# Softmax in a two-layer encoder trunk: dividing the value products instead of the probabilities, with reciprocals brought over the rows through DRAM

## The chip, the cores and the metric

The kernel runs on one core of a Trainium2 chip. The metric is device time in microseconds (us). Six places do the work: TensorE (PE, matmuls and transposes; PEld is its weight load), VectorE (DVE), ScalarE (ACT), GpSimd (POOL), SyncE (SP, which here issues every DMA) and the DMA engines. Each engine takes its own instructions in order; they wait for each other through semaphores.

## The reference

Two layers, 512 tokens, width 1024. Each layer has three attention branches of 8 heads with 64-wide values, a gated sum of them, and a feed-forward part. What matters here is the softmax and what follows it, the same in all branches:

```python
p = jax.nn.softmax(jnp.where(mask, s, NEG_INF), axis=-1)
outs.append(jnp.einsum('bhqk,bkhd->bqhd', p.astype(v.dtype), v[:, :q1]))
...
proj = jnp.einsum('bsnc,ncd->bsnd', y, w_branch[l])
gates = jax.nn.sigmoid(gl + b_gate[l]).reshape(B, S, N_BRANCH, D_MODEL)
merged = jnp.sum(gates * proj, axis=2)
x = x + merged @ w_out[l]
```

Branch 0 masks frame by frame and adds a forgetting bias, branch 1 (latent attention) masks by chunk, branch 2 adds a relative-position bias.

## The kernel before, in words

Matrix operands are kept as pairs: a rounded high part and the remainder ("hi"/"lo", `whi`/`wlo`, `yh`/`yl`), so that one product is three matmuls. Each weight tile is loaded by SP (`raw`), rounded by ACT (`whi`, L140) and its remainder taken by DVE or POOL (`wlo`, L142), with three buffers of each.

In a layer the branches come in the order 0, 2, 1. Attention goes head by head. For head h, `scores` handles four blocks of 128 queries in the order i = 3, 2, 1, 0 (512 to 128 keys each): PE makes `ps_s`; in branch 0 POOL first adds the diagonal mask to the bias tile `cb` (L665); DVE adds bias and score and takes the row's extreme (L670); ACT takes the exponential and its row sum `ls` (L675); DVE takes the reciprocal of the sum (L676) and multiplies the block of probabilities `pr` by it (L677). Then `probs` transposes the blocks on PE (`ps_p`, L689) and ACT and DVE split them (`pth` L691, `ptl` L692); `values` multiplies them with the values (`ps_y`, L700), so that features stand on partitions and queries on columns. The upper half of `ps_y` holds the low part of the values; ACT copies it (L704), DVE adds it (L709) and writes 64 partitions of the pair's tile `y`. After the odd head of a pair, ACT rounds it to `yh` (L712) and DVE takes the rest `yl` (L713). The next pair's queries and keys are transposed (`ps_q` L583), split (`nat` L585 on ACT, L586 on DVE) and, in branches 0 and 2, stacked by 12 DMAs (`qq`, `kk`, `kl`, L598). `nat` has three buffers, and a pair needs four, so that the fourth split waits until `qq` has read the first.

The order of the work on PE is written out by hand (the table `seq` in TUNE): scores of head h are interleaved with transposes and value products of head h-1, and between any two steps `Fill` puts matmuls that do not depend on the softmax: gate projections (`ps_f`) and branch projections (`ps_b`). On the other engines and in SP's queue the order is set by a scheduler that places instructions by its own estimates of times. Scratch tiles of 128x512 (`tmp`, shown as `t`) rotate through six buffers.

Of the kernel before, what the change touches and what calls it, by code (L numbers as in the profile page):

```python
# [9 lines left out]
F32 = mybir.dt.float32  # L10
# [3 lines left out]
ALU = mybir.AluOpType  # L14
# [4 lines left out]
P = 128  # L19
T = 512  # L20
# [4 lines left out]
H = 8  # L25
HD = 64
# [46 lines left out]
    head=1.0,  # L73
# [104 lines left out]
class Kern:  # L178
# [409 lines left out]
    def stacked(self, which, h, lo):  # L588
# [4 lines left out]
        def over(tag, first, second):  # L593
            s = self.tk(tag, [P, 2, T], F32R)
            for u in range(2):
                own, other = slice(HD * u, HD * u + HD), slice(HD - HD * u, P - HD * u)
                for rows, x in ((own, first), (other, second)):
                    nc.sync.dma_start(out=s[rows, u].bitcast(F32), in_=x[own].bitcast(F32))  # L598
            return s
# [2 lines left out]
            return over("kk", h, h), over("kl", lo, lo)  # L602
        return over("qq", h, lo), None

    def attention(self, l, branch, fill_ns, qkv):

        nc = self.nc
        yh, yl = [], []
        self.y = (yh, yl)
        per = 1 if branch == 1 else 2  # L610
        rows = KB if branch == 1 else P
        gc = (V_GA, V_GB, V_GC)[branch]
        qk, head = {}, {}
        if branch == 1:
            maskb = self.tk("maskb", [P, T], F32)
            nc.gpsimd.memset(maskb, 0.0)
            nc.gpsimd.memset(maskb[0:64, 448:512], BIG)
        else:
            cb = [self.tk("cb", [P, T], F32) for _ in range(2)]
        if branch == 2:  # L620
            for c in cb:
                nc.gpsimd.memset(c[0:64, 448:T], -BIG)

        def src(x, u):
            if branch == 1:
                return lambda t: x[t // 2][:, t % 2, u, :]
            return lambda t: x[t // 2][:, t % 2, u * P : (u + 1) * P]

        def transposed(u, which):
            x = qkv[which]  # L630
            if branch == 1:
                parts = [self.tk("st", [P, T], F32R) for _ in range(2)]
            else:
                parts = [self.tk("nat", [P, T], F32R) for _ in range(2)]
            self.feature_major(src(x, u), rows, self.gain(l, gc + which, 0, rows), parts)
            qk[u, which] = parts if branch == 1 else self.stacked(which, *parts)

        def begin(h):
            if branch == 1:
                bias = maskb  # L640
            else:
                bias = cb[h % 2]
                if branch == 0:
                    nc.sync.dma_start(out=bias, in_=self.cum[h : h + 1, :].to_broadcast([P, T]))
                else:
                    nc.sync.dma_start(out=bias[:, 0:448], in_=self.a["rel"][l, h, :, 0:448])
                    nc.sync.dma_start(out=bias[64:P, 448:T], in_=self.a["rel"][l, h, 64:P, 448:T])
            head[h] = dict(bias=bias, p=self.tk("pr", [P, 10 * P], F32))

        def scores(h, i):  # L650
            s = head[h]
            (qh, ql), (kh, kl) = qk[h // per, 0], qk[h // per, 1]
            if branch == 1:
                terms = [(a[0:KB], b[0:KB]) for a, b in ((qh, kh), (qh, kl), (ql, kh))]
            else:
                u = h % 2
                terms = [(qh[:, u], kh[:, u]), (qh[:, u], kl[:, u])]
            n = P * (i + 1)
            off = P * (i * (i + 1) // 2)
            ps = self.pS.tile([P, T], F32, tag="s", name="ps_s")  # L660
            for j, (a, b) in enumerate(terms):
                nc.tensor.matmul(out=ps[:, 0:n], lhsT=a[:, i * P : (i + 1) * P], rhs=b[:, 0:n], start=j == 0, stop=j == len(terms) - 1)  # L662
            if branch == 0:
                d = s["bias"][:, n - P : n]
                nc.gpsimd.tensor_tensor(out=d, in0=d, in1=self.maska, op=ALU.add)  # L665
            p = s["p"][:, off : off + n]
            b = s["bias"][:, 0:n] if branch == 0 else s["bias"][:, T - n : T]
            mn, ls, li = (self.small(1, x, 6) for x in ("mn", "ls", "li"))
            sign = 1.0 if branch == 2 else -1.0
            nc.vector.tensor_tensor_reduce(out=p, in0=ps[:, 0:n], in1=b, scale=1.0, scalar=-3e38 * sign, op0=ALU.add, op1=ALU.max if branch == 2 else ALU.min, accum_out=mn)  # L670
            if branch == 2:
                nm = self.small(1, "nm", 4)
                nc.vector.tensor_scalar(out=nm, in0=mn, scalar1=-1.0, scalar2=None, op0=ALU.mult)
                mn = nm
            nc.scalar.activation(out=p, in_=p, func=AF.Exp, bias=mn, scale=sign, accum_out=ls)  # L675
            nc.vector.reciprocal(out=li, in_=ls)  # L676
            nc.vector.tensor_scalar(out=p, in0=p, scalar1=li, scalar2=None, op0=ALU.mult)  # L677

        groups = (((0, 0),), ((1, 0), (3, 384)), ((2, 0),))
        offs = [0, P, 3 * P, 6 * P]  # L680

        def probs(h, gi):
            pr = head[h]["p"]
            ps = self.pt.tile([P, T], F32, tag="pt", name="ps_p")
            w = max(o + (NT - kb) * P for kb, o in groups[gi])
            for i in range(NT - 1, -1, -1):
                for kb, o in groups[gi]:
                    if kb <= i:
                        nc.tensor.transpose(ps[:, o + (i - kb) * P : o + (i - kb + 1) * P], pr[:, offs[i] + kb * P : offs[i] + (kb + 1) * P], self.ident)  # L689
            ph, pl = self.tk("pth", [P, T], F32R), self.tk("ptl", [P, T], F32R)  # L690
            nc.scalar.activation(out=ph[:, 0:w], in_=ps[:, 0:w], func=AF.Copy)  # L691
            nc.vector.tensor_tensor(out=pl[:, 0:w], in0=ps[:, 0:w], in1=ph[:, 0:w].bitcast(F32), op=ALU.subtract)  # L692
            head[h][gi] = (ph, pl)

        def values(h, gi, x):
            if gi == 0 and x == 0:
                head[h]["y"] = self.py.tile([P, T], F32, tag="y", name="ps_y")
            yps = head[h]["y"]
            for j, (kb, o) in enumerate(groups[gi]):
                nc.tensor.matmul(out=yps[:, kb * P : T], lhsT=qkv[2][kb // 2][:, kb % 2, h, :], rhs=head[h][gi][x][:, o : o + T - kb * P], start=gi == 0 and x == 0, stop=gi == 2 and x == 1)  # L700
            if gi < 2 or x == 0:
                return
            half = self.tmp()
            nc.scalar.activation(out=half[0:HD], in_=yps[HD:P], func=AF.Copy)  # L704
            if h % 2 == 0:
                head["y"] = self.tmp()
            y = head["y"]
            r0 = HD * (h % 2)
            nc.vector.tensor_tensor(out=y[r0 : r0 + HD], in0=yps[0:HD], in1=half[0:HD], op=ALU.add)  # L709
            if h % 2 == 1:  # L710
                a, b = self.ypool.tile([P, T], F32R, tag="yh", name="yh", bufs=4), self.ypool.tile([P, T], F32R, tag="yl", name="yl", bufs=4)
                nc.scalar.activation(out=a, in_=y, func=AF.Copy)  # L712
                nc.vector.tensor_tensor(out=b, in0=y, in1=a.bitcast(F32), op=ALU.subtract)  # L713
                yh.append(a)
                yl.append(b)
            del head[h]

        step = {
            "S": lambda h, i: scores(h, i),
            "P": lambda h, g: probs(h - 1, g),  # L720
            "V": lambda h, gx: values(h - 1, gx // 10, gx % 10),
            "T": lambda h, w: transposed(h // per + 1, w),
        }
        plan = []
        for h in range(H + 1):
            for op, arg, ns in TUNE["seq"]:
                if op == "T" and not (h % per == 0 and h // per + 1 < H // per):
                    continue
                if op == "S" and h == H or op in "PV" and h == 0:
                    continue  # L730
                plan.append((h, op, arg, ns * (TUNE["tail"] if h == H else TUNE["head"] if h == 0 else 1.0)))
        scale = fill_ns / sum(x[3] for x in plan)
        transposed(0, 0)
        yield 0.0
        transposed(0, 1)
        yield 0.0
        at = -1
        for h, op, arg, ns in plan:
            if h != at and h < H:
                begin(h)  # L740
            at = h
            step[op](h, arg)
            yield ns * scale
# [361 lines left out]
```

## Time and profile before

| | |
|---|---|
| median of three runs | 1857.61 us (1857.18 to 1859.98) |
| the profiled execution | 1858.96 us |
| its span, first to last instruction | 1856.9 us |
| mean granted TensorE clock | 0.993 |
| PE busy / DVE / ACT / POOL | 97% / 59% / 42% / 17% |

The page gives busy time by engine. The stretches of the attention branches are read off the timeline (times from the start of the span): in the first layer branch 0 stands at 74 to 178 us, branch 2 at 239 to 342, branch 1 at 437 to 513; in the second layer branch 0 at 995 to 1101, branch 2 at 1162 to 1265, branch 1 at 1362 to 1438. In the timelines and wait lists an idle time stands in square brackets or ahead of "times", with what ended it. "issue" of a DMA is the time that SP takes for it; "landing" is from issue until its data is there.

### The profile page before, as it was taken

The numbers are of one execution on the slowest core, as the hardware profiler recorded it, in microseconds if no ns is written. First come the engines' busy times: TensorE is split into PE (matmuls) and PEld (weight loads), VectorE is DVE, ScalarE is ACT, GpSimd is POOL, SyncE is SP. The second block draws the span as 40 slices with busy tenths as digits, with TensorE's granted clock in tenths as the row PEclk, the third lists the DMA queues.
The fourth block names the chain that finished last, engine by engine and source line by source line (L and its number), as shares of the span: only waits on it lengthen the run. The fifth ranks groups of instructions, "written<-read, shape, count | busy, mean of one in ns | idle before, by whom it ended". The sixth has DMA issues, their size and how long they took to land.

```text
span 1856.9 us, 23295 instructions
## 1 busy us (share of the span) xinstructions
PE 1801.5 (97%) x8496; PEld 1495.0 (81%) x8496; DVE 1088.9 (59%) x2223; ACT 784.5 (42%) x1369; POOL 311.4 (17%) x289
## 2 busy tenths in 40 slices
PE   8989989989999999999999899899899999999999
PEld 6778878877888888888887788788778888888887
DVE  7566468488865642454355654684888756334632
ACT  6565456446643221223245644564466433222221
POOL 1442222043101000000124312220431110000000
PEclk9999999999999999999999999999899999999999
DMA  5653365332252333333336533643322533333341
GB/s 180 154 147 105 101 163 138 100 113 69 80 193 80 106 99 98 96 100 110 119 113 158 132 96 109 169 116 110 103 84 80 178 95 97 102 91 102 92 119 62
DMA packets 78850, 211.46 MB, mean 114 GB/s; under 512 B 11392, under 2 KB 14464, under 8 KB 78736
## 3 DMA queue, kind: packets, MB, share of 16 engines
q1 hardware_dynamic: 78736, 209.97, 39.3%
q8 instruction: 67, 1.10, 0.2%
q14 instruction: 47, 0.39, 0.1%
HBM read 172.15 MB, written 12.62 MB: 100 GB/s over the span
## 4 chain that ended last, share of the span: by engine, by line
PE 79%; DVE 8%; ACT 4%; DMA 4%; issue 3%; POOL 2%; SPq 1%; DVEq 0%; ACTq 0%; POOLq 0%
PE ps L331 38%; PE ps_t L366 15%; PE ps_f L331 10%; PE ps_o L331 5%; PE ps_b L776 5%; PE ps_s L662 2%; PE ps_p L689 2%; PE ps_y L700 2%; DMA qq<-nat 2%; DVE pr L677 1%; POOL wlo L142 1%; DVE pr L670 1%; ACT whi L140 1%; DMA cb<-cum 1%; ACT pr L675 1%
## 5 line engine op out<-in xcount | busy, mean ns | idle before, releaser
L140 ACT ACTIVATE whi<-raw 128x1024 fp32r<-128x1024 f32 (+1 forms) x337 | 307.1, 919 | 764.8 <-issue 320.6
L142 DVE TENSOR_TENSOR wlo<-raw,whi 128x1024 fp32r<-128x1024 f32 (+2 forms) x237 | 287.6, 1213 | 232.2 <-ACT whi L140 227.8
L331 PE MATMUL ps<-xgh,whi 128*128 128x512 f32 x512 | 199.4, 389 | 0.0
L331 PE MATMUL ps<-xgh,wlo 128*128 128x512 f32 x512 | 199.2, 389 | 0.0
L331 PE MATMUL ps<-xgl,whi 128*128 128x512 f32 x512 | 199.2, 389 | 0.0
L331 PE MATMUL ps<-ah,whi 128*128 128x512 f32 x512 | 199.2, 389 | 0.0
L331 PE MATMUL ps<-al,whi 128*128 128x512 f32 x512 | 199.2, 389 | 0.0
L331 PE MATMUL ps<-ah,wlo 128*128 128x512 f32 x512 | 199.2, 389 | 0.0
L331 PE MATMUL ps_f<-xgh,whi 128*128 128x512 f32 x464 | 196.2, 423 | 0.0
L331 PE MATMUL ps_f<-xgh,wlo 128*128 128x512 f32 x464 | 182.5, 393 | 0.0
L331 PE MATMUL ps_f<-xgl,whi 128*128 128x512 f32 x464 | 182.5, 393 | 0.0
L142 POOL TENSOR_TENSOR wlo<-raw,whi 128x1024 fp32r<-128x1024 f32 x50 | 121.1, 2422 | 257.0 <-ACT whi L140 234.3
L366 PE MATMUL ps_t<-whi,xgh 128*128 128x512 f32 x384 | 151.2, 394 | 7.0 <-ACT whi L140 7.0
L366 PE MATMUL ps_t<-wlo,xgh 128*128 128x512 f32 x384 | 150.1, 391 | 0.0
L366 PE MATMUL ps_t<-whi,xgl 128*128 128x512 f32 x384 | 149.9, 390 | 0.0
L283 POOL TENSOR_TENSOR acc<-acc,t 128x512 f32<-128x512 f32 x24 | 41.6, 1732 | 518.9 <-ACT t L282 518.9
L331 PEld LDWEIGHTS ps<-ah,whi 128*128 128x128 f32 x512 | 96.1, 188 | 20.1
L331 PEld LDWEIGHTS ps<-xgl,whi 128*128 128x128 f32 x512 | 96.1, 188 | 19.9
L331 PEld LDWEIGHTS ps<-xgh,wlo 128*128 128x128 f32 x512 | 96.1, 188 | 19.9
L331 PEld LDWEIGHTS ps<-al,whi 128*128 128x128 f32 x512 | 96.1, 188 | 19.9
L331 PEld LDWEIGHTS ps<-xgh,whi 128*128 128x128 f32 x512 | 96.1, 188 | 19.9
L331 PEld LDWEIGHTS ps<-ah,wlo 128*128 128x128 f32 x512 | 96.1, 188 | 19.8
(194 smaller groups left out, 3387.0 us busy)
## 6 DMA issues: line engine op xcount, KB each, us to landing
raw<-w SPq DMA_DIRECT2D x277, 512.0 KB, 3.6
qq<-nat SPq DMA_DIRECT2D x64, 128.0 KB, 2.9
kk<-nat SPq DMA_DIRECT2D x64, 128.0 KB, 2.4
kl<-nat SPq DMA_DIRECT2D x64, 128.0 KB, 2.4
gd<-t SPq DMA_DIRECT2D x32, 256.0 KB, 2.2
cb<-cum SPq DMA_DIRECT2D x16, 256.0 KB, 4.0
cb<-gd SPq DMA_DIRECT2D x16, 256.0 KB, 2.7
g<-gd SPq DMA_DIRECT2D x16, 256.0 KB, 4.3
```

The costliest lines, as they stand in the source:

```text
L140: nc.scalar.activation(out=hi[:, c : c + v], in_=raw[:, c : c + v], func=AF.Copy)
L142: k.lo_engine.tensor_tensor(out=lo[:, c : c + w], in0=raw[:, c : c + w], in1=hi[:, c : c + w].bitcast(F32), op=ALU.subtract)
L283: (engine or nc.gpsimd).tensor_tensor(out=self.acc, in0=self.acc, in1=sq, op=ALU.add)
L331: nc.tensor.matmul(out=ps, lhsT=a[:, k], rhs=b[k], start=first and k == 0 and j == 0, stop=last and k == n - 1 and j == 2)
L366: nc.tensor.matmul(out=pss[t][:, 0:width], lhsT=a[k][:, t * P : t * P + P], rhs=b[:, i], start=c == 0 and i == 0 and j == 0, stop=last and ...
L662: nc.tensor.matmul(out=ps[:, 0:n], lhsT=a[:, i * P : (i + 1) * P], rhs=b[:, 0:n], start=j == 0, stop=j == len(terms) - 1)
L670: nc.vector.tensor_tensor_reduce(out=p, in0=ps[:, 0:n], in1=b, scale=1.0, scalar=-3e38 * sign, op0=ALU.add, op1=ALU.max if branch == 2 els ...
L675: nc.scalar.activation(out=p, in_=p, func=AF.Exp, bias=mn, scale=sign, accum_out=ls)
L677: nc.vector.tensor_scalar(out=p, in0=p, scalar1=li, scalar2=None, op0=ALU.mult)
L689: nc.tensor.transpose(ps[:, o + (i - kb) * P : o + (i - kb + 1) * P], pr[:, offs[i] + kb * P : offs[i] + (kb + 1) * P], self.ident)
L700: nc.tensor.matmul(out=yps[:, kb * P : T], lhsT=qkv[2][kb // 2][:, kb % 2, h, :], rhs=head[h][gi][x][:, o : o + T - kb * P], start=gi == 0 ...
L776: nc.tensor.matmul(out=pss[u], lhsT=chunk[a][:, u, k], rhs=y[b][k], start=k == 0 and j == 0, stop=k == 3 and j == 2)
```

## The change

The reciprocals per block (L676) and the multiplications of the probabilities (L677) go. ACT writes the row sums of both heads of a pair into one tile of 128x8. After the last block of the odd head, `pair_scale` takes the reciprocal of all eight columns on DVE, SP stores them to a DRAM row per head (1024 elements of 4 bytes, whose places in DRAM lie 4 bytes apart from partition to partition and 512 bytes apart from column to column), and two further DMAs read each row back, broadcast over 64 partitions, into a 128x512 tile `scale`. Once the pair's `y` is complete it is multiplied by `scale`: on POOL for the first three pairs of a branch, on DVE for the last. Line numbers below L605 grow by 11 to 17 in the changed kernel.

```diff
+    def pair_scale(self, h, head):
+        nc = self.nc
+        li = self.small(8, "li", 2).rearrange("p (u t) -> p u t", u=2)
+        nc.vector.reciprocal(out=li, in_=self.sums)
+        nc.sync.dma_start(out=self.rows[h - 1 : h + 1].rearrange("u (t p) -> p u t", p=P), in_=li)
+        scale = head[h]["scale"] = self.tmp()
+        for u in range(2):
+            nc.sync.dma_start(out=scale[HD * u : HD * u + HD], in_=self.rows[h - 1 + u : h + u, :].to_broadcast([HD, T]))
...
+            if h % 2 == 0:
+                self.sums = self.small(8, "ls", 2).rearrange("p (u t) -> p u t", u=2)
...
-            mn, ls, li = (self.small(1, x, 6) for x in ("mn", "ls", "li"))
+            mn = self.small(1, "mn", 6)
+            ls = self.sums[:, h % 2, i : i + 1]
...
             nc.scalar.activation(out=p, in_=p, func=AF.Exp, bias=mn, scale=sign, accum_out=ls)
-            nc.vector.reciprocal(out=li, in_=ls)
-            nc.vector.tensor_scalar(out=p, in0=p, scalar1=li, scalar2=None, op0=ALU.mult)
+            if h % 2 == 1 and i == 0:
+                self.pair_scale(h, head)
+
+        self.rows = self.dr.tile([H, T], F32, name=f"rows{l}_{branch}")
...
             if h % 2 == 1:
+                (nc.gpsimd if h + 1 < H else nc.vector).tensor_tensor(out=y, in0=y, in1=head[h]["scale"], op=ALU.mult)
```

The scheduler's order moves with it. On DVE, branch 0 of the first layer, the end of head 2; `ISA` is the bias-and-extreme instruction with its readout. Before:

```order
L670 ISA pr,mn<-ps_s,cb 128x256
L670 ISA mn 128x1
L586 SCALAR_TENSOR_TENSOR nat<-ps_q,vec,nat 128x512
L676 RECIPROCAL li<-ls 128x1
L677 TENSOR_SCALAR pr<-pr,li 128x256
L692 TENSOR_TENSOR ptl<-ps_p,pth 128x256
L586 SCALAR_TENSOR_TENSOR nat<-ps_q,vec,nat 128x512
L670 ISA pr,mn<-ps_s,cb 128x128
L670 ISA mn 128x1
L676 RECIPROCAL li<-ls 128x1
L677 TENSOR_SCALAR pr<-pr,li 128x128
```

And after:

```order
L684 ISA pr,mn<-ps_s,cb 128x256
L684 ISA mn 128x1
L586 SCALAR_TENSOR_TENSOR nat<-ps_q,vec,nat 128x512
L708 TENSOR_TENSOR ptl<-ps_p,pth 128x256
L684 ISA pr,mn<-ps_s,cb 128x128
L684 ISA mn 128x1
L586 SCALAR_TENSOR_TENSOR nat<-ps_q,vec,nat 128x512
L768 TENSOR_TENSOR mg_206<-ps_f,rb 128x512
```

The second `nat`, the one that waits for a `qq` DMA, stood ahead of the last score block and now stands behind it.

In SP's queue, the same place (end of head 1, start of head 2). `raw` is a weight tile, `cb` the bias of a later head, `qq` and `kk` the next pair's stacks. Before:

```order
L137 DMA raw_1572<-w 128x1024
L644 DMA cb_706<-cum0_397 128x512
L137 DMA raw_1690<-w 128x1024
L598 DMA qq_1112<-nat_1103 64x512 x2
L598 DMA qq_1112<-nat_1104 64x512 x2
L598 DMA kk_1146<-nat_1137 64x512 x4
```

And after, where `li` is the tile of reciprocals and `t2` the scale tile:

```order
L655 DMA cb_706<-cum0_397 128x512
L611 DMA rows0_0_707<-li_995 128x8x1
L137 DMA raw_1498<-w 128x1024
L614 DMA t2_998<-rows0_0_707 64x512 x2
L137 DMA raw_1607<-w 128x1024
L598 DMA qq_1081<-nat_1072 64x512
L598 DMA qq_1081<-nat_1073 64x512
```

The first weight load moved behind the bias load and the store of the reciprocals, and the two reads of the rows, which wait until that store has landed, stand ahead of the second weight load and of `qq`.

On ACT, at the pair's end in the same branch (start of head 3's steps on PE), after the change; `t_1013` is `y`, which POOL now multiplies just before:

```order
L707 ACTIVATE pth<-ps_p 128x512
L689 ACTIVATE pr,ls<-pr,mn 128x512
L729 ACTIVATE yh<-t_1013 128x512
L707 ACTIVATE pth<-ps_p 128x512
L689 ACTIVATE pr,ls<-pr,mn 128x384
```

One of the two splits of head 2's probabilities, which stood both behind `yh` before, now stands ahead of it; the other still stands behind.

## Rows read from the trace of the kernel before

**Rows 1.** The page, busy time of engines: us, share, instructions.

```profile
PE 1801.5 (97%) x8496; PEld 1495.0 (81%) x8496; DVE 1088.9 (59%) x2223; ACT 784.5 (42%) x1369; POOL 311.4 (17%) x289
```

**Rows 2.** Stretches: length, busy of PE, PEld, DVE, ACT, POOL, clock, DMA, GB/s.

```profile
74.00:178.00 104.00, 96.97 (x504) 79.29 (x504) 70.15 (x185) 63.42 (x140) 36.04 (x40) 1.00 0.53 133
239.00:342.00 103.00, 96.20 (x500) 80.23 (x500) 75.54 (x222) 59.13 (x135) 22.19 (x11) 0.98 0.54 140
437.00:513.00 76.00, 75.95 (x438) 64.81 (x438) 61.80 (x165) 52.10 (x122) 11.98 (x5) 1.00 0.26 77
...
995.00:1101.00 106.00, 97.48 (x497) 79.28 (x497) 69.89 (x184) 62.55 (x140) 35.94 (x40) 0.98 0.49 129
...
1162.00:1265.00 103.00, 96.22 (x502) 80.19 (x501) 76.34 (x222) 59.38 (x136) 22.21 (x11) 0.98 0.53 140
```

**Rows 3.** Waits of PE: total us, times, longest.

```profile
PE ps_p L689 <- DVE pr L677: 15.0, 14, 2.6
...
PE ps_y L700 <- DVE ptl L692: 7.1, 5, 2.1
```

**Rows 4.** Timeline of PE, matmuls that waited, branches 0 and 2.

```profile
113.02 0.33 PE L689 MATMUL ps_p<-ident,pr 128*128 128x128 f32 x1 [1.09 <-DVE pr L677]
...
118.86 0.50 PE L700 MATMUL ps_y<-ptl,v 128*128 128x512 f32 x1 [1.49 <-DVE ptl L692]
...
136.21 0.39 PE L700 MATMUL ps_y<-ptl,v 128*128 128x256 f32 x1 [1.79 <-DVE ptl L692]
...
278.22 0.33 PE L689 MATMUL ps_p<-ident,pr 128*128 128x128 f32 x1 [2.64 <-DVE pr L677]
```

**Rows 5.** DVE's groups by line: count, busy us, mean ns, idle before.

```profile
L677 DVE TENSOR_SCALAR pr<-pr,li 128x512 f32<-128x512 f32 x192 | 98.7, 515 | 5.4
...
L676 DVE RECIPROCAL li<-ls 128x1 f32<-128x1 f32 x192 | 30.4, 159 | 38.4 <-ACT pr L675 38.1
```

**Rows 6.** Timeline of DVE, branch 0: start, us, instruction.

```profile
101.50 0.49 DVE L677 TENSOR_SCALAR pr<-pr,li 128x512 f32<-128x512 f32 x1
...
110.96 0.75 DVE L586 SCALAR_TENSOR_TENSOR nat<-ps_q,vec,nat 128x512 fp32r<-128x512 f32 x1 [2.39 <-DMA qq<-nat]
...
115.77 1.83 DVE L677 TENSOR_SCALAR pr<-pr,li 128x512 f32<-128x512 f32 x1
```

**Rows 7.** Timeline of POOL at the same place.

```profile
114.92 2.40 POOL L142 TENSOR_TENSOR wlo<-raw,whi 128x1024 fp32r<-128x1024 f32 x1
```

**Rows 8.** DMAs by kind: count, KB each, median us to landing.

```profile
gd<-t SPq DMA_DIRECT2D x32, 256.0 KB, 2.2
cb<-cum SPq DMA_DIRECT2D x16, 256.0 KB, 4.0
...
cb<-rel SPq DMA_DIRECT2D x16, 16.0 KB, 2.8
```

**Rows 9.** The page, DMA queue: packets, MB, share of 16 engines.

```profile
q1 hardware_dynamic: 78736, 209.97, 39.3%
```

**Rows 10.** Timeline of ACT, head 1's last exponential in branch 0.

```profile
98.34 0.40 ACT L675 ACTIVATE pr<-pr,mn 128x128 f32<-128x128 f32 x1 [0.89 <-DVE mn L670]
```

**Rows 11.** Timeline of SP's queue around head 2 of branch 0.

```profile
95.63 0.34 SPq L137 DMA_DIRECT2D raw<-w  x1
...
105.43 0.33 SPq L137 DMA_DIRECT2D raw<-w  x1
105.85 2.40 SPq L598 DMA_DIRECT2D qq<-nat  x4
```

**Rows 12.** The page, POOL's 128x512 additions: count, busy us, mean ns.

```profile
L283 POOL TENSOR_TENSOR acc<-acc,t 128x512 f32<-128x512 f32 x24 | 41.6, 1732 | 518.9 <-ACT t L282 518.9
```

**Rows 13.** Timeline of DVE at the end of branch 1.

```profile
506.08 0.16 DVE L676 RECIPROCAL li<-ls 128x1 f32<-128x1 f32 x1
...
516.72 0.69 DVE L713 TENSOR_TENSOR yl<-t,yh 128x512 fp32r<-128x512 f32 x1 [0.70 <-ACT yh L712]
```

**Rows 14.** Timeline of PE, first matmul that needs branch 1's last remainder.

```profile
517.82 0.39 PE L776 MATMUL ps_b<-yl,whi 128*128 128x512 f32 x1
```

## The prediction

> **What bounds the kernel now.** First the page: PE is busy for 1801.5 of 1856.9 us [rows 1], so whatever the change frees on other engines, it can return only the 55.4 us in which PE stands idle, and what PE loses at a lowered clock. Then the table of stretches, to see how much of that lies where the change works. Length minus PE's busy time is 7.0 and 8.5 us in the two stretches of branch 0, 6.8 us in each of branch 2, and 0.05 us in branch 1 [rows 2]: 29.1 us in all, and branch 1 has nothing to give. In three of the four stretches with idle time the mean clock is 0.98; 0.02 x (103 + 106 + 103) = 6.2 us. So 35 us is the most that could come back.
>
> The waits of PE say what ends these idle times. The multiplication of the probabilities ends 15.0 us of them in 14 waits, the split `ptl` 7.1 us in 5 [rows 3]. The timeline shows two mechanisms behind them. The first is DVE's own work: at 118.86 PE waited 1.49 us for `ptl` [rows 4], which stood behind a multiplication of 128x512 that took 1.83 us instead of the 0.49 us of its like at 101.50 [rows 6]; during it POOL ran a 2.40 us subtraction [rows 7]. The second is a DMA: at 110.96 a `nat` split ended a 2.39 us wait for `qq` [rows 6], the last score block of the head was queued behind it, and PE waited 1.09 us at 113.02 for that block's multiplication; the waits of 1.79 at 136.21 and 2.64 at 278.22 are of this kind [rows 4].
>
> **What the change removes.** 192 multiplications (98.7 us) and 192 reciprocals (30.4 us) leave DVE [rows 5]; 24 reciprocals of 128x8 and 6 products come. DVE is busy 67% of branch 0 and 73% of branch 2, so this is worth nothing by itself. What counts is where DVE was the last to come:
> - Waits for the multiplication, 15.0 us. The transposes now take the block straight from ACT's exponential, and the last score block stands ahead of the waiting `nat` in the place that the order shows. I keep 2 us for exponentials that come late: -13.
> - Waits for `ptl`. The wait of 1.49 us and its counterpart in the second layer (the two stretches are alike) go with the long multiplication: -3. The ones like 136.21 stay, since that `ptl` still stands behind `nat`.
> - Clock: I count about two thirds of the 6.2 us, on the view that most dips follow the long waits that go: -4.
>
> Together -20 us, bounds 0 (all covered by something that comes equally late) and -35.
>
> **What it adds.** Per pair SP issues three more DMAs, 72 in all, at about 0.6 us each (four `qq` in 2.40 us [rows 11]): 43 us of a queue that is mostly waiting. What matters is their order. SP stops at the two reads of the rows until the store has landed, and `qq` stands behind them.
>
> How long that store takes, L, no row shows: 1024 pieces of 4 bytes, 64 per engine. Lower bound: a 256 KB store to DRAM lands in 2.2 us, and a 16 KB load in 64 pieces of 256 bytes in 2.8 [rows 8]. Upper bound: the queue's packets took 39.3% of 16 engines' span for 78736 of them [rows 9], 0.393 x 16 x 1856.9 / 78736 = 0.148 us each, with 2.7 KB in a mean packet; 64 of those are 9.5 us, plus 2.2 for the way of any store 11.7. Between 2.2 and 11.7 no row is clearly nearer, so I take the geometric mean, L = 5.
>
> The Trainium skill speaks against the store: DMA: Bandwidth & Descriptors, section Rules for kernel authors, says that a non-contiguous last dimension becomes one descriptor per element and asks to rearrange it. The same page's Measured table has 4 KB in 64 packets at 0.68 us; by that figure the descriptors are cheap, L would be an estimated 2.9 us (0.68 above the 2.2 us row), the scale would be there in time at the end of branch 1, and the forecast would be about 1 us lower. No run here shows either yet.
>
> With L = 5, at head 2 of branch 0: the exponential ends at 98.34 + 0.40 with its readout behind [rows 10], the reciprocal and SP's issue bring the store to about 99.3, it lands at 104.3, and the two reads end at 105.5. The weight load and `qq` stood at 105.43 and 105.85 before [rows 11], so the reads alone cost nothing. But the weight load of 95.63 now stands behind the store, 4 us later, and the next one, which waits until POOL has used a buffer, may come up to 1.8 us later with it. I call this the A-place: two pairs in each stretch of branch 0, four times about 1 us: +4, bounds 0 and 7. In branch 2 the order puts the second load behind the stacks, so `qq` has some room there.
>
> POOL's product stands between `y` and `yh`. The nearest row is POOL's addition of the same shape, 1.73 us [rows 12]: 18 of them, 31 us. POOL has the time (36 of 104 us busy [rows 2]), but ACT, which runs in order, meets `yh` with one `pth` behind it, for which PE waits soon. The order puts `yh` one split later than before, which covers most of the 1.73 us if POOL is not then in a 2.40 us subtraction. I take 0.17 us per place: +3, bounds 0 and 31.
>
> At the end of branch 1 nothing covers the product on DVE. `yl` ended at 516.72 + 0.69 = 517.41 [rows 13], and PE needed it at 517.82 [rows 14]: 0.41 us of room. A product of the same shape on DVE costs the same 0.69 us, so PE loses 0.3. The scale must also be there: reciprocal at 506.08 [rows 13], store landed at 511.4, reads issued by 512.6, landed by 516.6 (4.0 us for a broadcast row [rows 8]), against `y` just before 516. That makes about 1 us per layer: +2, bounds 0 and 14.
>
> **Sum.** Against the profiled execution: 1858.96 - 20 + 4 + 3 + 2 = 1848.0. That execution lies 1.35 us above the median of the runs, so I predict 1847 us, 0.6% faster. Its own range, with each term halved or raised by half, is 1838 to 1854.
>
> **Rivals.**
> 1. *The queue behind the store.* If L is long, SP holds `qq` back. From L = 5.4 `qq` is late; DVE's second `nat` and all behind it wait longer. I give it 2 us of room, because the last score block no longer stands behind `nat`, so that PE pays from L = 7.4: eight places (two pairs, branches 0 and 2, two layers) and two ends of branch 1, 10 us for each us of L. It breaks even with the gain at L = 8.5. At L = 9.3 it gives 1847 + 19 = 1866, at the upper bound 1890. For it: the 0.148 us per packet; against it: those packets are 600 times larger. This is the case that ends slower. Chance 0.21.
> 2. *New waits take the place of the old.* ACT stands at `yh` while POOL finishes a subtraction and then the product (up to 2.40 + 1.73 us after `y`), and `pth` is late in its place. In branches 0 and 2 there are 12 such places; with 0.9 us each, 11 us, the gain is gone: 1857. For it: POOL's subtractions run in all these stretches, and the scheduler knows the traffic only by estimates. Against: the splits moved ahead of `yh`. Chance 0.19.
> 3. *All of it comes.* L near the lower bound, no new waits, all dips of the clock and the waits for `ptl` gone as well: 1857.6 - 25 = 1833. Against it: the waits for `qq` remain by construction. Chance 0.08.
>
> My forecast has chance 0.52. Against no change counts what a measurement of this kernel can tell, 0.2% or 3.7 us. Faster: the forecast, nearly all of rival 3 and a few hundredths of rival 2, 0.61. Same: most of rival 2 and the edges of the forecast and of rival 1, 0.18. Slower: rival 1 and a little of rival 2, 0.21. The range leaves out most of rival 3 below and the worse half of rival 1 above: 1835 to 1864.
>
> **What would show it.** In the changed profile: no wait of PE for DVE's multiplication, idle time of the four stretches of branches 0 and 2 down from 29 to about 15 us, their clock nearer to 1.00. The store's landing at 4 to 6 us; `qq` at most 2 us later than before relative to the heads. `yh` on ACT waiting for POOL by no more than a few tenths of a us; a wait of about 1 us of PE where branch 1's last `yh` and `yl` are first used. The forecast is wrong if the store lands later than about 8 us, if idle time of PE appears within branch 1, or if PE's waits merely change their releaser from DVE to ACT or DMA at the same sum.

## The result, and the profile after

The changed kernel takes 1954.17 us (median of 4 runs, 1952.13 to 1954.41), the kernel before 1858.44 us on the same chip: a ratio of 1.0512, 95% interval 1.0494 to 1.0531. The forecast was 1847 us with a range up to 1864. It was wrong in its sign and far outside its range.

First the page of the changed kernel, the parts that answer to [rows 1, 9]: busy time of the engines, and the DMA queue.

```profile
PE 1827.6 (94%) x8496; PEld 1512.4 (77%) x8496; DVE 991.4 (51%) x1869; ACT 785.5 (40%) x1369; POOL 333.1 (17%) x307
...
q1 hardware_dynamic: 107536, 216.37, 42.9%
```

The span is 1952.3 us, 95.4 longer. PE's idle time, span minus busy time, is 124.7 us instead of 55.4: 69.3 of the 95.4. The other 26.1 are PE's own busy time, for the same 8496 matmuls: they ran at a lower clock (mean 0.971). DVE lost 97.5 us of work, as the change set out to do, and the time that this freed went unused. The queue has 28,800 packets more.

Where the time went is in the table of stretches (us, busy time of PE, PEld, DVE, ACT, POOL, granted clock, DMA share, GB/s). The borders are set so that about as many matmuls lie in each as in [rows 2] (in branch 1 467 and 461 instead of 438), so they lie later: branches 0, 2 and 1 of the first layer, then of the second.

```profile
74.00:192.00 118.00, 101.04 (x505) 84.01 (x504) 52.50 (x125) 63.31 (x140) 39.28 (x43) 0.93 0.64 116
253.00:374.00 121.00, 101.28 (x499) 83.48 (x498) 58.35 (x161) 59.43 (x134) 26.02 (x14) 0.90 0.61 119
468.00:568.00 100.00, 85.45 (x467) 70.63 (x465) 52.70 (x120) 55.85 (x125) 15.82 (x8) 0.96 0.33 80
1048.00:1166.00 118.00, 102.00 (x514) 84.01 (x513) 54.94 (x127) 64.84 (x142) 39.49 (x44) 0.94 0.62 116
1228.00:1348.00 120.00, 101.17 (x501) 83.40 (x500) 58.77 (x161) 58.69 (x133) 23.62 (x13) 0.91 0.60 124
1440.00:1540.00 100.00, 86.85 (x461) 71.59 (x460) 53.56 (x121) 55.32 (x123) 15.82 (x8) 0.95 0.39 97
```

Length minus PE's busy time is 13 to 20 us in every one of the six, 99 us together, and the clock is down to 0.90 to 0.96. Branch 1, which had 0.05 us of idle time, now has 14.6 and 13.2.

The waits of PE (total us, times, longest), as [rows 3], among those of the engines that it depends on:

```profile
POOL t L727 <- DMA t<-rows: 73.5, 8, 15.4
...
DVE nat L586 <- DMA qq<-nat: 61.8, 10, 10.0
...
PE ps_y L716 <- DVE ptl L708: 34.4, 6, 7.4
...
ACT yh L729 <- POOL t L727: 31.5, 12, 5.2
...
PE ps_b L793 <- ACT yh L729: 13.2, 2, 7.0
PE ps_p L705 <- DVE nat L586: 11.6, 4, 6.0
```

and, among the waits of SP's queue, that at the reads of the rows:

```profile
SPq L614 <- DMA rows<-li: 219.8, 24, 11.8
```

The multiplication ends no wait of PE any more; that part came as forecast. In its place stand waits that go back, as the runs below show, to one transfer: SP stood 219.8 us at the 24 pairs of reads, until the store had landed. The DMAs by kind (count, KB each, median us from issue to landing) give its time, and show that others are slower too: the gate's store `gd<-t` was at 2.2 us in [rows 8].

```profile
gd<-t SPq DMA_DIRECT2D x32, 256.0 KB, 4.2
...
rows<-li SPq DMA_DIRECT2D x24, 4.0 KB, 10.9
```

One place shows how it works, head 2 of branch 0, the place of [rows 11]. SP's timeline (start, us, instruction):

```profile
97.34 0.37 SPq L611 DMA_DIRECT2D rows<-li  x1
98.73 0.34 SPq L137 DMA_DIRECT2D raw<-w  x1
106.83 1.12 SPq L614 DMA_DIRECT2D t<-rows  x2
108.04 0.54 SPq L137 DMA_DIRECT2D raw<-w  x1
108.67 3.32 SPq L598 DMA_DIRECT2D qq<-nat  x4
```

and the stretches of 4 us around it (columns as above; the last two are the DMA share and GB/s):

```profile
100.00:104.00 4.00, 3.72 (x22) 2.92 (x21) 2.87 (x6) 3.95 (x9) 1.35 (x3) 1.00 0.49 15
104.00:108.00 4.00, 4.00 (x25) 3.45 (x24) 1.82 (x5) 2.83 (x8) 2.83 (x2) 1.00 0.53 31
108.00:112.00 4.00, 4.00 (x23) 3.40 (x22) 0.38 (x3) 2.24 (x5) 0.45 (x1) 1.00 0.88 194
112.00:116.00 4.00, 0.94 (x5) 0.42 (x3) 0.00 (x0) 0.00 (x0) 1.92 (x1) 1.00 1.04 209
116.00:120.00 4.00, 1.08 (x5) 1.08 (x6) 1.85 (x3) 0.50 (x1) 0.00 (x0) 0.56 0.63 138
```

From 100 to 108 us only 15 to 31 GB/s are moved. The trace also records every single DMA packet (its start, length and bytes), and these records tell what stands there. The 1024 pieces last 9 ns each (median), and nearly all of them have started by 100 us. Behind them comes the weight load issued at 98.73: its first 15 packets of 4 KB start between 99.7 and 100.7 us and last 2.2 to 8.5 us, where the median packet of that size lasts 0.16. So the DMA engines are not busy with pieces during these 8 us; other packets hang while the store has not landed. In branch 1 there is a place where SP has nothing else on the way. Between the pieces and the landing the DMA engines do nothing at all there (SP's timeline, and a stretch of 4 us in the columns above):

```profile
477.78 0.38 SPq L611 DMA_DIRECT2D rows<-li  x1
489.00 1.42 SPq L614 DMA_DIRECT2D t<-rows  x2
```

```profile
482.00:486.00 4.00, 4.00 (x26) 3.55 (x26) 2.52 (x7) 3.71 (x10) 2.40 (x1) 1.00 0.00 0
```

Back at head 2 of branch 0: when the store has landed, the load, the two reads, a second load and the four `qq` come out together at 194 to 209 GB/s, `qq` last. DVE's second split waited for it, and PE for that split; between 116 and 120 the mean granted clock falls to 0.56 (0.50 is the level of 1.2 GHz, 1.00 that of 2.4), after PE had stood idle; its whole wait, until 118.92, was 5.98 us:

```profile
118.11 0.75 DVE L586 SCALAR_TENSOR_TENSOR nat<-ps_q,vec,nat 128x512 fp32r<-128x512 f32 x1 [9.66 <-DMA qq<-nat]
```

```profile
118.92 1.11 PE L705 MATMUL ps_p<-ident,pr 128*128 128x128 f32 x4 [5.98 <-DVE nat L586]
```

The counterpart of that DVE row waited 2.39 us [rows 6].

The theories tested: (1) SP stands in order at the reads, so what is issued behind them is late. (2) The pieces in the DMA rings (the queues of the DMA engines) make what is queued behind the store late even where no engine waits for it. (3) The product on POOL in front of `yh`, and the order that the scheduler makes around it, hold ACT up.

### The profile page after: what moved, and what is told of

Read it like the earlier page. It is cut to its first block, busy times and chain, and to the rows that moved or that the text cites. A ratio compares the mean times of both kernels' runs of the same rounds, so it can differ in the third digit from the quotient of the medians.

```text
span 1952.3 us, 23165 instructions
## 1 busy us (share of the span) xinstructions
PE 1827.6 (94%) x8496; PEld 1512.4 (77%) x8496; DVE 991.4 (51%) x1869; ACT 785.5 (40%) x1369; POOL 333.1 (17%) x307
## 3 DMA queue, kind: packets, MB, share of 16 engines
q1 hardware_dynamic: 107536, 216.37, 42.9%
## 4 chain that ended last, share of the span: by engine, by line
PE 70%; DMA 15%; DVE 6%; ACT 4%; issue 2%; SPq 1%; POOL 1%; DVEq 0%; POOLq 0%; ACTq 0%
PE ps L331 36%; PE ps_t L366 14%; DMA rows<-li 9%; PE ps_f L331 8%; PE ps_o L331 4%; PE ps_b L793 4%; DMA qq<-nat 2%; DMA t<-rows 2%; PE ps_s L675 1%; PE ps_p L705 1%; PE ps_y L716 1%; DMA cb<-cum 1%; ACT pr L689 1%; SPq L598 1%; ACT whi L140 1%
## 5 line engine op out<-in xcount | busy, mean ns | idle before, releaser
L331 PE MATMUL ps_f<-xgh,whi 128*128 128x512 f32 x464 | 201.9, 435 | 0.0
L331 PE MATMUL ps_f<-xgl,whi 128*128 128x512 f32 x464 | 187.2, 404 | 0.0
L331 PE MATMUL ps_f<-xgh,wlo 128*128 128x512 f32 x464 | 186.6, 402 | 0.0
L708 DVE TENSOR_TENSOR ptl<-ps_p,pth 128x512 fp32r<-128x512 f32 x144 | 85.3, 599 | 60.7 <-ACT pth L707 59.8
```

Of the source, the lines that this page charges most:

```text
L331: nc.tensor.matmul(out=ps, lhsT=a[:, k], rhs=b[k], start=first and k == 0 and j == 0, stop=last and k == n - 1 and j == 2)
```

## The experiments

All times are medians; the kernel before was between 1858.59 and 1859.57 us in each set.

### The store alone: how many pieces, of what size

*The packed store.* The reciprocals go out in 32 contiguous bytes per partition.

```
-  out=self.rows[h-1:h+1].rearrange("u (t p) -> p u t", p=P), in_=li
+  out=self.rows[h-1:h+1].rearrange("u (p t) -> (u p) t", t=8), in_=li.rearrange("p u t -> p (u t)")
```

> The store of the reciprocals writes 128 pieces of 32 contiguous bytes instead of 1024 pieces of 4 bytes; the instructions of every engine stand in the same order as in the changed kernel. The reciprocals come back in another order, so the scaling is not the reference's. Theory 1 (SP waits in order at the two reads until a store of 1024 pieces has landed, and the loads and stacks behind it are late): the store lands in 2.5 to 4 us instead of 10.9, SP's waits at the reads fall from 219.8 us to about 70, DVE's waits of nat for qq fall from 61.8 us to about 20, time 1840 to 1865. Theory 2 (not SP's order but the pieces in the DMA rings slow the other transfers): the same time here, so this run does not tell 1 from 2. Theory 3 (the product on POOL in front of yh, and the order that the scheduler makes around it, holds ACT up): time stays above 1920.

Measured: 1833.57 us, ratio 0.9863 (0.9848 to 0.9878), 120 us below the changed kernel, by nothing but the shape of 24 small stores. Theory 3 is out as the cause of the loss. The time is even below what theories 1 and 2 gave. The store's row among this run's DMAs, and DVE's wait for `qq`:

```profile
rows<-li SPq DMA_DIRECT2D x24, 4.0 KB, 1.8
```

```profile
DVE nat L586 <- DMA qq<-nat: 16.0, 9, 5.8
```

PE is busy for 1793.2 of 1833.0 us: idle 39.8 us instead of 55.4, and busy 8.3 us less for the same matmuls, with a mean clock of 0.996. The largest of PE's waits that are left in branches 0 and 2 are 4.1 us for `kl` and 3.3 us for `nat`, in four waits each.

*256 pieces, with the scale read in the order in which it was stored.*

```
-  out=self.rows[h-1:h+1].rearrange("u (t p) -> p u t", p=P)
+  out=self.rows[h-1:h+1].rearrange("u (p t) -> p u t", t=4)
-  out=y, in0=y, in1=scale
+  out=y as "q t p", in0=y as "q t p", in1=scale.rearrange("q (p t) -> q t p", t=4)
```

> The store writes 256 pieces of 16 contiguous bytes (row, partition, block) and the product on POOL or DVE reads the scale with a stride of 4 elements, so that the result is the reference's; the order of all instructions is that of the changed kernel. If the landing time goes by the number of pieces, 10.9 us for 1024 and 1.8 us for 128 give about 2.9 to 3.2 us for 256, and the time is that of the packed store plus at most a few us for the strided product: 1833 to 1842. Rival: POOL's product with a stride of 16 bytes takes twice as long and holds yh up in 18 places, 1850 to 1860.

Measured: 1838.85 us, ratio 0.9896 (0.9881 to 0.9911), landing 2.6 us. The strided product took 1.56 us on POOL instead of 1.29, and 1.07 instead of 0.69 on DVE: the rival's price was far too high. This is the change's idea in a form that computes the same division and beats both kernels, by 1.0% and 5.9%.

*512 pieces of 8 bytes, 1024 of 8 and 512 of 4.* The first by a row laid out `(a p b)` with b = 2, the second with each reciprocal written twice, the third by storing only the first head's row. The order is the change's, but for a few instructions of DVE, ACT and SP in e13:

```
e8   out=self.rows[h-1:h+1].rearrange("u (a p b) -> p (u a) b", p=P, b=2)
e13  li is 128x16, each value twice; the same rows, twice as long
e14  out=self.rows[h-1:h].rearrange("u (t p) -> p (u t)", p=P), in_=li[:, 0, :]
```

> The store in 512 pieces of 8 bytes, in the changed kernel's order (the reciprocals come back in another order, so the scaling is not the reference's). By the number of pieces, 10.9 us for 1024 and 2.6 for 256 put its landing at 5.4 us; by the forecast's price of 10 us for each us of landing above 7.4 it would be no slower than 1850.

> The changed kernel with each reciprocal written twice, so that the store has 1024 pieces of 8 bytes (the values come back in another order and twice, the scaling is not the reference's). If the number of pieces decides, it lands in 10 to 11 us as 1024 pieces of 4 bytes do, and the time is about 1950; if pieces of 4 bytes are dear, it lands in twice the 4.3 us of 512 pieces of 8 bytes less the fixed part of about 1 us, 7 to 8 us, and the time is between 1845 and 1900.

> The changed kernel, its order kept, with only the first head's row stored, in 512 pieces of 4 bytes; both reads take that row (the second head of a pair is scaled by the first one's reciprocals). If the number of pieces decides, 4.3 us as 512 pieces of 8 bytes, time 1837 to 1845; if pieces of 4 bytes are dear, 5.5 to 6 us, time up to 1850.

The store's row in these three, in this order:

```profile
rows<-li SPq DMA_DIRECT2D x24, 4.0 KB, 4.3
```

```profile
rows<-li SPq DMA_DIRECT2D x24, 8.0 KB, 5.5
```

```profile
rows<-li SPq DMA_DIRECT2D x24, 2.0 KB, 8.5
```

The last column but one counts the packets of other transfers that lasted over 2 us, by the trace's packet records; the kernel before has none.

| store | landing, us | SP's wait at the reads, us | packets over 2 us | time, us |
|---|---|---|---|---|
| 128 pieces of 32 bytes | 1.8 | 29.2 | 0 | 1833.57 |
| 256 of 16 | 2.6 | 38.6 | 6 | 1838.85 |
| 512 of 8 (one run) | 4.3 | 73.4 | 45 | 1841.34 |
| 1024 of 8 (two runs) | 5.5 | 93.4 | 30 | 1842.48 |
| 512 of 4 (two runs) | 8.5 | 171.2 | 199 | 1928.38 |
| 1024 of 4 (the change) | 10.9 | 219.8 | 276 | 1954.17 |

The ratios of the last two new ones are 0.9915 (0.9883 to 0.9947) for 1024 pieces of 8 bytes and 1.0377 (1.0344 to 1.0411) for 512 of 4. My expectation of 7 to 8 us for 1024 pieces of 8 bytes was too high, and that of 5.5 to 6 for 512 pieces of 4 too low; both err on the same side. It is the piece of 4 bytes that is dear: 512 of them take longer than 1024 of 8. The DMA engines do not spend that time on the pieces. By the packet records a piece lasts 9 ns in all six, and 97% of a store's pieces have started 1.6 to 2.2 us after its issue (medians), whether it lands in 1.8 us or in 10.9. What differs comes after that, until the writes have landed; no record follows a write that far, so why is not settled. Neighbouring partitions write neighbouring pieces in every one of these stores, so the size of a piece and its distance in DRAM are not told apart either. And the time hardly moves up to a landing of 5.5 us (9 us more than with 1.8), then jumps by 86 us on the way to 8.5.

### What the removal and the product are worth

*No division at all*, and *the product alone*, by a constant tile:

```
-            if h % 2 == 1 and i == 0:
-                self.pair_scale(h, head)
-                ... tensor_tensor(out=y, in0=y, in1=head[h]["scale"], op=ALU.mult)     (e3: left out)
+                ... tensor_tensor(out=y, in0=y, in1=self.ones broadcast, op=ALU.mult)  (e4)
```

> Reciprocals, store, reads and product are all left out (the division is not done at all): what the removal of the 192 multiplications and 192 reciprocals is worth alone. My prediction's term of -20 us puts it at 1839, with bounds 1824 and 1859. Rival: the waits for the multiplication are replaced by equally late exponentials and qq, and it stays within 1855 to 1862. If it comes out above 1862, the removal itself costs, through the order the scheduler makes, and all three theories on the added part are too small.

> The pair's values are multiplied on POOL (the last pair on DVE) as in the changed kernel, but by a constant tile of ones; no reciprocal, no store, no reads (the division is left out). Theories 1 and 2: as without any division plus my term of +3 us for the product in front of yh, 1838 to 1848. Theory 3: most of the loss is here, 1900 or more.

Measured: 1847.02 (ratio 0.9934, 0.992 to 0.9949) and 1851.18 (0.9961, 0.9946 to 0.9975). Both are slower than the packed store, which does more. The groups of PE's matmuls told why; here one of the feed-forward's, in the run without division:

```profile
L331 PE MATMUL ps<-ah,whi 128*128 128x512 f32 x512 | 201.7, 394 | 0.0
```

Every other run so far had 389 ns there, far from anything that was changed. These two kernels lack the small tiles `li`, and all tiles allocated behind them start 64 bytes earlier. So both ran again with the padding tile 64 bytes wider (`pad` 56 to 72 columns), instructions and order the same:

> As the run without any division, in the same order, but with the small pool padded by 64 bytes, so that the tiles behind it (ah, mh, yh, pth and others) start 96 bytes past a multiple of 128 as in the kernel before and the changed one, not 32 bytes past it. If the 394 ns of the matmuls on ah and mh in the run without division (389 in all the others) come from where the tiles start, they return to 389 and the time falls by 9.9 us to about 1837. If they come from the values (no division makes them other ones) or the order, it stays at 1847.

> The product by a constant tile of ones alone (the division is left out), padded in the same way. By the start of the tiles: 394 ns return to 389 and it falls from 1851 to about 1841, 3 to 5 us above the padded run without division, which is then the price of the product. Else it stays at 1851.

```profile
L331 PE MATMUL ps<-ah,whi 128*128 128x512 f32 x512 | 199.2, 389 | 0.0
```

Measured: 1834.67 (0.9872, 0.985 to 0.9895) and 1838.07 (0.9895, 0.9875 to 0.9916). The padding alone is worth 12 and 13 us, so it was the place of the tiles. The matmuls on `ah`, `al`, `mh` and `ml` account for 9.9 us of it, those on `yh` and `yl`, which moved too, for 2 to 3 more. The removal alone gives 24.3 us. The product costs 3.4 of them, but the two intervals overlap, so the 3.4 is not clear of noise.

### SP's wait, or the rings

*Reads that do not wait*: the two reads take a row of `cum`, written long before, once with the change's store (e5) and once with the packed one (e5c).

```
-  in_=self.rows[h - 1 + u : h + u, :].to_broadcast([HD, T])
+  in_=self.cum[h - 1 + u : h + u, :].to_broadcast([HD, T])
```

> Reciprocals, the store of 1024 pieces and the product are those of the changed kernel; the two broadcast reads take a DRAM row that was written long before, so that SP never waits for the store (the values are scaled by other numbers than the reciprocals). Theory 1: the store still lands in about 11 us, but nothing waits for it: DVE's waits of nat for qq fall from 61.8 us to about 20, time 1838 to 1858. Theory 2: the pieces are still in the rings, qq and the gate's stores still land late, time stays above 1900. Theory 3: above 1900.

> As the run whose reads do not wait for the store (they take a DRAM row written long before, so the values are scaled by other numbers), in the same order, but the store writes 128 pieces of 32 bytes instead of 1024 of 4. Theory 2 (the pieces themselves hold up what stands behind them in the DMA rings, though no engine waits for the store): falls from 1896 to 1834 to 1845, the gate's stores land in 2.2 us again instead of 6.1. Rival: the other place of the reads in SP's order, or the product, costs the 62 us above the packed store; then it stays at 1880 to 1896.

Measured: 1895.58 us (ratio 1.0196, 1.018 to 1.0211) and 1837.82 us (0.9895, 0.9878 to 0.9912). With the two others:

| | 1024 pieces of 4 bytes | 128 of 32 |
|---|---|---|
| the reads wait for the store | 1954.17 | 1833.57 |
| the reads do not wait | 1895.58 | 1837.82 |

Neither theory alone holds. The store in pieces costs 58 us though no engine waits for it (e5 and e5c have the same order). Another 59 us lie between e5 and the change. They are not SP's wait alone: in e5 the scale is never late either, and DVE, ACT, POOL and SP have another order. With few pieces wait and order together cost nothing (1833.57 against 1837.82).

PE runs its matmuls in one order in all these kernels, so their stretches can be compared matmul for matmul. By how many us they are longer than in the kernel before, both layers together:

| | branch 0 | branch 2 | branch 1 | the 66 us behind branch 1 |
|---|---|---|---|---|
| the change | 22.3 | 35.5 | 20.3 | 19.4 |
| the reads do not wait (e5) | 18.7 | 20.6 | -0.9 | 2.8 |

So without the wait nothing is lost in branch 1, and two thirds of what the wait adds lie in and behind it, where no `qq` is stacked. There the weight loads stand behind the reads in SP's queue, and the scale itself is late: POOL waits for it, ACT for POOL's product, and at the end PE for `yh`. No run separates the two.

What the store does to others shows in the DMAs of the run in which nobody waits for them:

```profile
kk<-nat SPq DMA_DIRECT2D x64, 128.0 KB, 3.5
...
gd<-t SPq DMA_DIRECT2D x32, 256.0 KB, 6.1
...
g<-gd SPq DMA_DIRECT2D x16, 256.0 KB, 6.8
```

With the packed store and the same order the three are at 2.4, 2.1 and 3.3 us, and no packet lasts over 2 us, against 281 here. The Trainium skill says (DMA: Bandwidth & Descriptors, section Queues, rings and completion order) that each DMA engine takes its descriptors in ring order; no run here shows that, since no record names the engine of a packet. The packets that hang show that waiting for a turn is not all of it: by the records they had started.

*The kernel before with the store added, unread*: the eight reciprocals of a pair are gathered in one small tile and stored, the division stays as it was.

```
-  li = self.small(1, "li", 6)
+  li = self.lis[:, 4 * (h % 2) + i : 4 * (h % 2) + i + 1]
   ...
+  if h % 2 == 1 and i == 0: store of self.lis into rows that nobody reads  (e9: 1024 pieces; e9b, e9c: 128)
```

> The kernel before, division and all, with one thing added: in each pair the eight reciprocals are also stored to DRAM in 1024 pieces of 4 bytes, in the changed kernel's place; nobody reads them, SP waits for nothing more. Theory 2 (the pieces hold up what stands behind them in the rings): the two runs whose reads do not wait differ by 58 us, 1896 against 1838, for the same 24 stores, so 1859 + 58 = 1917 here, between 1890 and 1935. Theory 1 alone (only SP's wait counts): 1859 to 1865.

> The same with the store in 128 pieces of 32 bytes: both theories 1857 to 1864. If this too is 1880 or more, it is not the pieces but the store's place or the issue on SP.

> The kernel before plus the unread packed store, with the small pool padded by 128 bytes so that the tiles behind it start where they do in the kernel before (224 past a multiple of 256 instead of 96). Matmuls on ah and mh return from 395 to 389 ns, 11.4 us less: 1864. If the store itself cost the 16 us, it stays near 1875.

Measured: 1923.45 (ratio 1.0342, 1.0323 to 1.036), 1875.19 (1.0088, 1.0073 to 1.0103) and 1859.67 (1.0005, 0.9995 to 1.0016). e9b missed its expectation by 11 us, again by the place of the tiles (matmuls on `ah` at 395 ns); with the padding of e9c, 389 ns, it takes the time of the kernel before. The three have the order of the kernel before, with the 24 stores put in. So a packed store that nobody reads costs nothing, and the same 4 KB in pieces of 4 bytes cost 48 us in the pair that shares its places (e9 against e9b): the effect that theory 2 names, from the side of the kernel before. Here too the packets tell the two apart: 211 last over 2 us in e9, none in e9b.

*SP's wait without pieces*: the packed store, then three dependent copies of the rows within DRAM ahead of the reads.

```
+  for k in range(3):
+      nc.sync.dma_start(out=self.rows[k + 1, h-1 : h+1], in_=self.rows[k, h-1 : h+1])
```

> The packed store, and then three copies of the two rows from DRAM to DRAM, each waiting for the one before, ahead of the two reads: SP stands for a chain of about 8 to 10 us, but with few pieces in the rings (128 and three times 16). The order has some of the stacks ahead of the last copy. Theory 1 (SP's wait costs by itself): after against the run whose reads do not wait is 58 us, so 1834 + 58 = 1892, at least 1860. Theory 2 alone: 1834 to 1845.

Measured: 1924.25 us (ratio 1.0344, 1.0323 to 1.0365), 32 us above theory 1's figure and within its "at least 1860", but inconclusive. The scheduler made another order around the 72 copies. DVE waited for `qq` only 14.0 us, no packet lasted over 2 us, and PE's largest wait is one that stays below 1 us in the other runs, for DVE to read out the one buffer of `ps_y`:

```profile
PE ps_y L718 <- DVE t L727: 61.0, 24, 3.6
```

## Why the prediction was wrong

*The step that failed* is the store's landing time L. No row showed it; I bounded it by 2.2 and 11.7 us and took 5. It was 10.9, inside the bounds. The mean of two ends was no reason for 5. The figure of the Trainium skill (DMA: Bandwidth & Descriptors, section Measured), by which I estimated 2.9 us, pointed further away still: the run has 10.9. The page gives it for loads, and I used it for a store. The rule of the Trainium skill (same page, section Rules for kernel authors), that a non-contiguous last dimension becomes one descriptor per element and should be rearranged, spoke against the change, and the packed store's 1.8 us agree with it. The upper bound's own reason does not hold either, so that 10.9 lies near it by luck: it priced a packet at 0.148 us, the trace's 4-byte packets last 9 ns, and 1024 packets of 8 bytes land in 5.5 us. Both bounds looked for the time in the pieces; it was spent behind them.

*The price of a late landing* failed too. Rival 1 was the right mechanism, but it let PE pay from L = 7.4 at 10 us per us, which gives 1858 at L = 8.5 and 1882 at 10.9. Measured are 1928 and 1954. Two things were left out. The wait was counted at ten places (eight where `qq` stands behind the reads, and the two ends of branch 1), but the store also holds up other transfers where no engine waits for it: 58 us, nearly all in branches 0 and 2. And branch 1 was priced only at its end: there the weight loads, the gate's stores and the product wait, ACT stands at `yh`, and 14.6 and 13.2 us were idle where next to nothing had been; branch 1 and what follows it lost 39.7 us in all.

The other steps, each against its run:
- Removal, -20 (0 to -35): 24.3 us without any division. Right; the term was 4 us too small.
- Product in front of `yh`, +3 (0 to 31): 3.4 us, not clear of noise. Nothing speaks against the term. The trace has 1.29 us for one product where I took 1.73 [rows 12].
- A-place +4 and end of branch 1 +2: with the packed store nothing is left of them; that run is 4.5 us below the product alone, with intervals that just touch. At a landing of 5.5 us the kernel takes 1842.48, so these late places and the reads together are worth 9 us over a landing of 1.8; I had 6.
- The sum: at the L that I assumed it was near. 1842.48 at 5.5 us against a forecast of 1847, own range 1838 to 1854. That range does not come out of its rule: with all terms halved or all raised by half the sum gives 1852 or 1841, with gain and costs moved against each other 1832 or 1861.
- Clock, -4: with the packed store the mean clock does rise to 0.996. In the changed kernel it fell instead, and 26.1 us of the loss are PE's slower matmuls.
- Rival 3, "all of it comes", gave 1833 for L near its lower bound. The packed store landed in 1.8 us and took 1833.57. What I held against it was right and did not count: DVE still waited 16.0 us for `qq` (16.8 before), but the last score block no longer stood behind that wait, and PE waited only 3.3 us in all for `nat`.

Of the signs that I named, the missing wait for the multiplication came; the idle time of the four stretches went to 71.5 us, not 15; `qq` was late by far more than 2 us; `yh` waited 31.5 us for POOL instead of tenths of a us at a place. Two of the three signs named for a wrong forecast came: a landing above 8 us, and idle time within branch 1. The third, the same sum of waits with another releaser, did not: the sum grew.

Open: how the 59 us divide between SP's standing, the late scale and the order, since the run meant for it changed the order; and what happens to pieces of 4 bytes once they have left the DMA engines.

## What to carry to other kernels

Neither a transfer's size in bytes nor the time of its packets says what it costs: 4 KB in pieces of 4 bytes had left the DMA engines about 2 us after issue and landed after 10.9, and other transfers paid meanwhile, in a queue whose mean share rose only from 39.3 to 42.9%. A DMA share that is low or half full can thus hide a transfer that holds up all others; the time to landing shows it. Lay a small store out so that each partition writes a contiguous run, and undo the permutation in the operand of the next instruction, which cost 0.3 to 0.4 us per product here. Where a term of a sum has no row and its bounds lie on both sides of the verdict, the forecast is a statement on that term: measure it, or give the far end its full weight and price all that stands behind it, not only the places that come to mind.

## What the runs showed of the hardware

- Stores to DRAM, median landing by piece: 512 pieces of 4 bytes 8.5 us and 1024 of them 10.9 (9.6 in e9), against 4.3 and 5.5 for pieces of 8 bytes, 2.6 for 256 of 16 and 1.8 for 128 of 32 (2.1 to 2.5 in the other orders).
- These times are not spent in the DMA engines: a piece's packet lasts 9 ns in every shape, and nearly all have started about 2 us after issue. While such a store is on its way, packets of other transfers hang, up to 10.0 us in the changed kernel, where none lasts over 1.6 us in the kernel before.
- Where a matmul's operand tiles start changed its time. With `ah` at 224 bytes past a multiple of 256 the matmuls of 128x512 took 389 ns, at 160 past 394, at 96 past 395, over 1536 matmuls of the feed-forward, and 389, 396 and 395 over the 384 on `mh` and `ml`: 9.9 and 11.4 us per run. My expectation for the padded run put it on the multiple of 128; the case of 96 shows that this was too coarse. A change that adds or removes a small tile can so move the time by 0.7 to 0.8% without touching any path; four of the kernels here did.
- POOL's product of 128x512 took 1.29 us where its addition of the same shape takes 1.73 [rows 12], and 1.56 with one operand at a stride of 16 bytes.
